# The first 70 microseconds of a streaming encoder step: conditions by 128-column blocks and another order of loads and engines

## The chip, the cores and the metric

The kernel runs on one core of a Trainium2 chip. A core has a matrix engine (TensorE, PE in the profile, with PEld for its weight loads), a vector engine (VectorE, DVE), an activation engine (ScalarE, ACT), GpSimd (POOL) and a sync engine (SyncE, SP). Each engine works through its own list of instructions in order, and the lists wait for one another by semaphores. DMA transfers are issued from the lists of SP, ACT or POOL and run on 16 shared DMA engines. The metric is the device time of one execution in microseconds; the kernel before takes 2170.99 us (median of 3 runs, 2169.61 to 2173.06).

## The reference

One step of a two-layer encoder in float32, for a prompt of 1024 frames and a sample of 32 frames that share the weights; the model width D is 1024.

```python
def rmsnorm(x, g):
    y = xf * lax.rsqrt(jnp.mean(xf * xf, axis=-1, keepdims=True) + EPS)
    return (y * g).astype(x.dtype)
...
for i in range(DEPTH):
    mod = jax.nn.silu(c) @ w_ada[i] + b_ada[i]
    sh1, sc1, gt1, sh2, sc2, gt2 = jnp.split(mod[:, None, :], N_MOD, axis=-1)
    h = rmsnorm(x, g_norm[i, 0]) * (1 + sc1) + sh1
    ...   # layer 0: z = gelu(h @ w_in), u and v are its halves, v is normalised and mixed over positions
    x = x + gt1 * rmsnorm(mix, g_norm[i, 1])
    h = rmsnorm(x, g_norm[i, 2]) * (1 + sc2) + sh2
    f = jnp.square(jax.nn.relu(h @ ffn_w_up[i])) @ ffn_w_down[i]
    x = x + gt2 * rmsnorm(f, g_norm[i, 3])
```

What matters here is the start of layer 0: the condition vector c (one for the prompt, one for the sample) gives a shift sh1 and a scale sc1 of 1024 entries each through a 1024 x 1024 block of w_ada; x is normalised, scaled and shifted to h; h is multiplied with w_in, whose second half gives v.

## The kernel before, in words

The 1056 rows are held transposed, features on the 128 partitions, in three tiles of 384, 384 and 288 columns (TILES). The 1024 features are eight blocks, written k = 0 to 7 here. Each float32 product of activations and weights is made of three products of split values: every weight tile is split into a high part (wh, by ScalarE, do_w, L422) and a low part (wl, by VectorE, L79 by the helper tt), the activations into hh and hl, and TensorE sums high-high, high-low and low-high.

All loads stand in one list, `stream`, and are issued by SP in that order as far as buffers are free (`issue`, L395 to L416). A weight item ("w") lands in one of three raw buffers; the x blocks ("x") and the first condition slices ("ada") have places of their own. `stream_to(kind, key)` works the list off up to an item: for a weight the split, for an x block the sum of squares on ScalarE (x_squares, L565) and eight 128 x 128 transposes on TensorE with copies out on VectorE or ScalarE (x_turn, L580 to L588), for a condition slice `do_ada_pe`. The list begins with x blocks 0 to 2, then four rounds q = 0 to 3, each with two half slices of the scale, two of the shift and one item of the weight for v, ("v", 0, q), which holds features 2q and 2q+1 for the first 512 columns of v. x blocks 3 to 5 follow the first round, 6 to 8 the last.

Conditions, in the prologue: a slice is 256 of the 6144 columns of w_ada, loaded in two halves of 512 KB (512 features by 256 columns). Slices 0 to 3 give the shift sh1, slices 4 to 7 the scale sc1. `do_ada_pe` (L472) multiplies them on TensorE with the Silu of c in four column groups of the array, and VectorE transposes the result in 32 x 32 blocks (L489, tile adas). A `fold`, called later, gathers it on TensorE with a small matrix (L459, tile adat) and lets VectorE add the bias and, for a scale, multiply with the gain (ada_finish, tiles shift and coef). TensorE, in order, stands at the gather until the transpose is done.

`first_norm` (L887) is a generator. Its first step makes the root of the mean square (spread, L715 to L727: a Sqrt by ScalarE, a reciprocal and a Newton step by VectorE), its second spreads it over the partitions with a diagonal (L730) and a matmul with ones (L732, tile pb_h) and copies it out (L893). Each further step (apply, L857) makes two blocks k of the modulated activations: mt (VectorE), hh (ScalarE, L875), hl (VectorE). Such a block needs scale and shift of its k.

The projection to v begins while all this runs: `early_mm` (L961, matmuls at L973) takes five blocks of 128 rows, three of the first tile (0, 1, 2) and two of the second (3, 4), and for each round q first the products with wh, then those with wl. The order of the whole prologue (from L991) is written out by hand in a `tc.manual_schedule()`. Its loop for q = 0 to 3: the next two k of tile 0, early_mm of blocks 0 to 2; in the first round x blocks 3 to 5 and the norm of tile 1; the next two k of tile 1; then `conditions(q + 1)` (both slices of the next round and the first fold), the next weight item, early_mm of block 3, the second fold, early_mm of block 4. After the loop come x blocks 6 to 8 (the third tile), its norm, and the sixth block; from there a planner orders the work.

The small vectors (gains, biases, c, pool scale, v's gain) are rows loaded by `load_vectors` on ScalarE's queue and turned by TensorE (turn_conditions for c, with Silu at L194; turn_vectors for the others, L206).

Later, v_rms makes the same kind of root for v's norm, once per tile, at L1067.

Of the kernel before, what the change touches and what calls it, by code (L numbers as in the profile page):

```python
# [15 lines left out]
P = 128  # L16
# [8 lines left out]
NV = 2  # L25
# [9 lines left out]
def tile_stream_encoder_step(  # L35
# [144 lines left out]
    def load_vectors(i, part):  # L180
        at = sum(k for _, k in rows[i][: part.start])
        for ap, k in rows[i][part]:
            nc.scalar.dma_start(vec_rows[i][at : at + k, :P], ap)
            at += k
# [6 lines left out]
    def turn_conditions():  # L191
# [4 lines left out]
        act(out=raw[0:16, 2 * P : 2 * P + 1], in_=epsT[0:16, :], func=AF.Sqrt)  # L196
# [50 lines left out]
    def add_wide(l, j):  # L247
# [10 lines left out]
                (2, 512),  # L258
            )
# [81 lines left out]
    for q in range(4):  # L341
# [3 lines left out]
        if q == 0:  # L345
            for b in range(3, 6):
                add_x(b)
# [33 lines left out]
    def in_raw(k):  # L381
        kind, key = stream[k][:2]
        return kind != "x" and not (kind == "ada" and k < first_ada)
# [11 lines left out]
    def issue():  # L395
        while state["issued"] < len(stream):
# [22 lines left out]
    def do_w(key, r):  # L419
# [4 lines left out]
        if key == ("v", 0, 0):  # L424
# [47 lines left out]
    def do_ada_pe(l, sl, q, r):  # L472
# [18 lines left out]
        def fold():  # L491
# [4 lines left out]
            )  # L496

# [111 lines left out]
    def stream_step():  # L609
# [6 lines left out]
        if kind == "w":  # L616
            do_w(key, r)
        elif kind == "wide":
# [96 lines left out]
    def spread(t, ss, tag, out, dg):  # L715
# [6 lines left out]
        act(out=r0[:, :nb], in_=ms[:, :nb], func=AF.Sqrt)  # L722
        nc.vector.reciprocal(out=r0[:, :nb], in_=r0[:, :nb])
# [129 lines left out]
    def apply(t, l, cf, sh, r, keep=False):  # L853
# [3 lines left out]
        if keep and len(segs[t]) == 1:  # L857
            parts = [parts[k] + parts[k + 1] for k in range(0, KB, 2)]
# [102 lines left out]
    def early_mm(bs, q):  # L961

        wh, wl = witem[("v", 0, q)]
        for second in (False, True):
            for b in bs:
                t, c0 = b // 3, b % 3 * P
                tick(0.46 if second else 0.92)
                for k in range(2):
                    kb = 2 * q + k
                    a_h, a_l = hh[t][:, kb, c0 : c0 + P], hl[t][:, kb, c0 : c0 + P]  # L970
                    w = slice(k * 512, k * 512 + 512)
                    for a in (a_h,) if second else (a_h, a_l):
                        mm(  # L973
                            early_ps[b],
                            a,
                            (wl if second else wh)[:, w],
                            start=kb == 0 and a is a_h and not second,
                            stop=kb == KB - 1 and second,
                        )
# [5 lines left out]
    def conditions(q):  # L985

        stream_to("ada", (0, 4 + q, 1))
        stream_to("ada", (0, q, 1))
        pe_folds.pop(0)()

    with tc.manual_schedule():  # L991
# [682 lines left out]
```

## Time and profile before

| | before |
|---|---|
| median of 3 runs | 2170.99 us (2169.61 to 2173.06) |
| profiled execution, whole time | 2173.74 us |
| its span, first to last instruction | 2171.7 us |
| granted TensorE clock, mean over the span | 0.996 |
| instructions | 33210 |
| HBM traffic over the span | 143 GB/s |

The profile is one execution. In lists of instructions a line reads: start, duration, engine, source line, operation, output<-inputs, form, count, and in brackets the idle time of the engine before it and what ended that. In the chain of waits a line is start, duration and what ran; "issue" is time in which nothing that the profile shows was waited for. In groups, the number after the bar is the busy time and the mean of one in ns, behind the second bar the idle time before them. In rows of stages the stretch is followed by its length, the busy time of PE, PEld, DVE, ACT and POOL with the number of instructions, the granted clock, the mean busy share of the DMA engines and GB/s. A row of waits is: engine and line, what it waited for, total us, times, longest. A row of DMA issues ends with KB of each and the median time to landing.

### The profile page before, as it was taken

Reading aid. Unit: us, or ns where it says so; the run is one execution under the profiler, and the core shown is the slowest. Engines: PE = TensorE matmul, PEld = TensorE weight load, DVE = VectorE, ACT = ScalarE, POOL = GpSimd, SP = SyncE. Lnnn points to the kernel's source line nnn. Section 1 sums busy time; section 2 is a strip of 40 time slices with the busy share of each in tenths; the row PEclk is TensorE's granted clock in tenths of the full one; section 3 lists DMA queues with packets and bytes.
Section 4 is the critical chain, followed back from the end, with each engine's and each line's share of the span. In section 5 each row is a group of like instructions: output and inputs, shape, how many; then the busy total and the mean of one; then the engine's idle time right before and its main releaser. Section 6 shows DMA issues by size and latency. Waiting matters only on the chain.

```text
span 2171.7 us, 33210 instructions
## 1 busy us (share of the span) xinstructions
PE 2145.5 (99%) x13214; PEld 2078.1 (96%) x13214; DVE 1431.8 (66%) x2499; ACT 971.3 (45%) x1643; POOL 13.3 (1%) x30
## 2 busy tenths in 40 slices
PE   7999999999999999999999999999999999999998
PEld 5778899999999999999999999999999999999997
DVE  5688647566879548496747879869675554523377
ACT  4633422234447552323445566666555542313354
POOL 0000000000000000000000000000000000000001
PEclk9999999999999999999999999999999999999999
DMA  8386534343437454243645466565455552302255
GB/s 300 119 269 193 173 93 139 90 148 109 147 96 233 132 155 143 87 140 110 196 129 161 141 189 182 171 191 158 141 161 158 157 155 68 98 20 78 69 139 125
DMA packets 383262, 312.95 MB, mean 144 GB/s; under 512 B 39458, under 2 KB 346346, under 8 KB 383108
## 3 DMA queue, kind: packets, MB, share of 16 engines
q1 hardware_dynamic: 380452, 308.64, 46.8%
q8 instruction: 103, 1.69, 0.3%
q10 hardware_dynamic: 2144, 1.41, 0.2%
q0 software_dynamic: 512, 0.79, 0.1%
q14 instruction: 51, 0.42, 0.1%
HBM read 278.95 MB, written 31.84 MB: 143 GB/s over the span
## 4 chain that ended last, share of the span: by engine, by line
PE 93%; DVE 3%; DMA 2%; ACT 1%; issue 1%; ACTq 0%; DVEq 0%; SPq 0%
PE pg L902 11%; PE pg L903 11%; PE pg L904 11%; PE pf L902 11%; PE pf L904 11%; PE pf L903 11%; PE po L902 3%; PE po L903 3%; PE po L904 3%; PE pu L902 3%; PE pu L904 3%; PE pu L903 3%; PE pv L929 2%; PE pv L930 2%; PE pv L931 2%; PE pp L1532 1%
## 5 line engine op out<-in xcount | busy, mean ns | idle before, releaser
L902 PE MATMUL pg<-fh,wh_dn 128*128 128x384 f32 (+1 forms) x1536 | 495.8, 323 | 0.0
L902 PE MATMUL pf<-hh,wh_up 128*128 128x384 f32 (+1 forms) x1536 | 494.4, 322 | 0.0
L903 PE MATMUL pf<-hl,wh_up 128*128 128x384 f32 (+1 forms) x1536 | 493.1, 321 | 0.0
L904 PE MATMUL pf<-hh,wl_up 128*128 128x384 f32 (+1 forms) x1536 | 492.9, 321 | 0.2 <-DVE wl_up L79 0.2
L903 PE MATMUL pg<-fl,wh_dn 128*128 128x384 f32 (+1 forms) x1536 | 492.6, 321 | 0.4 <-DVE fl L79 0.4
L904 PE MATMUL pg<-fh,wl_dn 128*128 128x384 f32 (+1 forms) x1536 | 492.5, 321 | 0.0
L79 DVE TENSOR_TENSOR wl_up<-raw,wh_up 128x1024 fp32r<-128x1024 f32 x152 | 185.9, 1224 | 165.4 <-ACT wh_up L422 165.4
L902 PEld LDWEIGHTS pg<-fh,wh_dn 128*128 128x128 f32 x1536 | 288.3, 188 | 1.5 <-ACT fh L1121 0.6
L903 PEld LDWEIGHTS pg<-fl,wh_dn 128*128 128x128 f32 x1536 | 288.3, 188 | 1.5 <-DVE fl L79 0.7
L904 PEld LDWEIGHTS pf<-hh,wl_up 128*128 128x128 f32 x1536 | 288.6, 188 | 0.5 <-DVE wl_up L79 0.5
L903 PEld LDWEIGHTS pf<-hl,wh_up 128*128 128x128 f32 x1536 | 288.3, 188 | 0.4
L902 PEld LDWEIGHTS pf<-hh,wh_up 128*128 128x128 f32 x1536 | 288.2, 188 | 0.4
L904 PEld LDWEIGHTS pg<-fh,wl_dn 128*128 128x128 f32 x1536 | 288.3, 188 | 0.0
L422 ACT ACTIVATE wh_up<-raw 128x1024 fp32r<-128x1024 f32 x152 | 161.2, 1060 | 279.9 <-PE pf L903 213.6
L79 DVE TENSOR_TENSOR acc<-acc,pg 128x384 f32<-128x384 f32 (+1 forms) x336 | 174.2, 519 | 146.3 <-PE pg L904 145.7
L422 ACT ACTIVATE wh_dn<-raw 128x1024 fp32r<-128x1024 f32 x152 | 160.8, 1059 | 202.9 <-PE pg L903 170.6
L79 DVE TENSOR_TENSOR wl_dn<-raw,wh_dn 128x1024 fp32r<-128x1024 f32 x152 | 186.0, 1224 | 82.4 <-ACT wh_dn L422 82.2
L79 DVE SCALAR_TENSOR_TENSOR aa<-raw,csil,aa 128x512 f32<-128x512 f32 (+1 forms) x364 | 203.5, 623 | 8.0 <-DMA raw<-in_w_ada_dram 7.9
L1295 ACT ACTIVATE r<-pf 128x384 f32<-128x384 f32 (+1 forms) x192 | 86.6, 451 | 201.9 <-PE pf L904 199.2
L79 DVE TENSOR_TENSOR fl<-r,fh 128x384 fp32r<-128x384 f32 (+1 forms) x192 | 100.3, 523 | 85.4 <-ACT fh L1121 84.3
L902 PE MATMUL pu<-hh,wh_u 128*128 128x384 f32 (+1 forms) x384 | 125.8, 328 | 0.0
L902 PE MATMUL po<-ush,wh_o 128*128 128x384 f32 (+1 forms) x384 | 123.5, 322 | 0.0
(263 smaller groups left out, 2927.2 us busy)
## 6 DMA issues: line engine op xcount, KB each, us to landing
raw<-in_ffn_w_up_dram SPq DMA_DIRECT2D x152, 512.0 KB, 3.9
raw<-in_ffn_w_down_dram SPq DMA_DIRECT2D x152, 512.0 KB, 3.5
raw<-in_w_ada_dram SPq DMA_DIRECT2D x96, 512.0 KB, 4.3
raw<-in_sgu_w_in_dram SPq DMA_DIRECT2D x40, 512.0 KB, 4.4
xd<-acc SPq DMA_DIRECT2D x8, 1536.0 KB, 7.8
raw<-in_sgu_w_out_dram SPq DMA_DIRECT2D x24, 512.0 KB, 4.0
xo_r<-xd SPq DMA_DIRECT2D x32, 384.0 KB, 3.4
vd<-vt SPq DMA_DIRECT2D x32, 256.0 KB, 4.5
```

The costliest lines, as they stand in the source:

```text
L79: return op(out, *args, **kw)
L422: act(out=wh, in_=r, func=AF.Copy)
L902: mm(ps[:, :n], wh, rh, start=i == 0, stop=False)
L903: mm(ps[:, :n], wh, rl, start=False, stop=False)
L904: mm(ps[:, :n], wl, rh, start=False, stop=i == last)
L929: mm(ps[:m, :], a_h, wh[:, o : o + 512], start=k == 0, stop=False)
L930: mm(ps[:m, :], a_h, wl[:, o : o + 512], start=False, stop=False)
L931: mm(ps[:m, :], a_l, wh[:, o : o + 512], start=False, stop=k == KB - 1)
L1295: act(out=r[:, :n], in_=ps[:, :n], func=AF.Relu)
L1532: mm(ps[:, :n], wg[:, k, e * P : (e + 1) * P], A(t, 2 * g + k), start=k == 0, stop=k == 1)
```

## The change

It touches the prologue up to the third tile's norm, and one line of v_rms.

- Shift and scale of k = 0 and k = 1 come from four blocks of 128 columns (columns 8, 0, 9, 1, each one load of 512 KB with all 1024 features), in place of slices 4 and 0. A new function, do_col, multiplies such a block.
- The order of loads: x 0 to 2; columns 8 and 0; ("v", 0, 0); columns 9 and 1; round 1; x 3 to 5; rounds 2 and 3; x 6 to 8. x block 2 is issued by SP instead of ScalarE's queue.
- g_norm, b_ada, pool_scale and sgu_g_v are issued by GpSimd's queue; c_prompt and c_sample stay on ScalarE's. A Silu of one column stands before the real one.
- Sqrt and reciprocal become Abs_reciprocal_sqrt, in spread and in v_rms.
- apply takes k = 0 and k = 1 one at a time. The low parts of all four items of v's first columns are made when the order calls for them (late_lo).
- The hand-written order is another one, and early_mm takes a list of k and either the products with wh or those with wl.

```diff
-    def load_vectors(i, part):
+    def load_vectors(queue, i, part):
...
-        act(out=raw[0:16, 2 * P : 2 * P + 1], in_=epsT[0:16, :], func=AF.Sqrt)
+        act(out=raw[0:16, 2 * P : 2 * P + 1], in_=epsT[0:16, :], func=AF.Abs_reciprocal_sqrt)
...
-    for q in range(4):
+    add_col(KB)
+    add_col(0)
+    add_w(*v_item(0, 0))
+    add_col(KB + 1)
+    add_col(1)
+    for q in range(1, 4):
         for j in (8 + 2 * q, 9 + 2 * q, 2 * q, 2 * q + 1):
             add_ada(0, j)
         add_w(*v_item(0, q))
-        if q == 0:
+        if q == 1:
             for b in range(3, 6):
                 add_x(b)
...
-                i = (nc.scalar if key == 2 else nc.sync).dma_start(
+                i = nc.sync.dma_start(
...
-        if key == ("v", 0, 0):
+        if key[:2] == ("v", 0):
...
+    def do_col(l, f, r):
+        pa = ps_ms(f"ada{l}_c{f}")
+        for k in range(KB):
+            c = k % 4
+            mm(
+                pa[32 * c : 32 * c + 32, :P],
+                csil32[:, k, :],
+                r[:, k * P : (k + 1) * P],
+                start=k < 4,
+                stop=k >= 4,
+                tile_position=(0, 32 * c),
+                skip_group_check=True,
+            )
+        s = t_m(f"adas{l}_c{f}")
+        nc.vector.transpose(out=s[:, :P], in_=pa[:, :P])
...
-        act(out=r0[:, :nb], in_=ms[:, :nb], func=AF.Sqrt)
-        nc.vector.reciprocal(out=r0[:, :nb], in_=r0[:, :nb])
+        act(out=r0[:, :nb], in_=ms[:, :nb], func=AF.Abs_reciprocal_sqrt)
...
-            parts = [parts[k] + parts[k + 1] for k in range(0, KB, 2)]
+            parts = parts[:2] + [parts[k] + parts[k + 1] for k in range(2, KB, 2)]
...
     with tc.manual_schedule():
-        load_vectors(2, slice(0, 2))
+        load_vectors(nc.scalar, 2, slice(0, 2))
         issue()
...
+        load_vectors(nc.gpsimd, 0, slice(0, 1))
+        load_vectors(nc.gpsimd, 1, slice(0, 1))
+        load_vectors(nc.gpsimd, 2, slice(2, 4))
+        act(out=vec_rows[2][64:80, P : P + 1], in_=epsT[64:80, :], func=AF.Silu)
         turn_conditions()
...
+        stream_to("x", 2)
         turn_vectors()
         next(h0)
+        column(KB)
+        fold()
+        column(0)
         statistics(h0)
+        fold()
         stream_to("w", ("v", 0, 0))
+        next(h0)
+        early_mm(front, (0,), False)
+        late_lo.pop()()
+        column(KB + 1)
+        early_mm(front, (0,), True)
+        fold()
+        column(1)
+        fold()
+        next(h0)
+        early_mm(front, (1,), False)
+        early_mm(front, (1,), True)
+        slice_(5)
+        fold()
+        slice_(1)
+        fold()
+        stream_to("w", ("v", 0, 1))
+        next(h0)
+        early_mm(front, (2, 3), False)
+        late_lo.pop()()
+        early_mm(front, (2, 3), True)
+        stream_to("x", 5)
+        turn_x()
+        next(h1)
+        slice_(6)
+        statistics(h1)
+        fold()
+        next(h1)
+        next(h1)
+        early_mm(rear, (0, 1), False)
+        early_mm(rear, (0, 1), True)
+        slice_(2)
+        fold()
+        stream_to("w", ("v", 0, 2))
+        next(h0)
+        next(h1)
+        early_mm(front, (4, 5), False)
+        late_lo.pop()()
+        early_mm(rear, (2, 3), False)
+        early_mm(rear, (2, 3), True)
+        early_mm(front, (4, 5), True)
+        next(h1)
+        slice_(7)
+        fold()
+        slice_(3)
+        fold()
+        early_mm(rear, (4, 5), False)
+        early_mm(rear, (4, 5), True)
+        stream_to("w", ("v", 0, 3))
+        next(h0)
+        next(h1)
+        early_mm(front, (6, 7), False)
+        late_lo.pop()()
+        early_mm(rear, (6, 7), False)
+        early_mm(front, (6, 7), True)
+        early_mm(rear, (6, 7), True)
         stream_to("x", 8)
...
-        act(out=x, in_=m, func=AF.Sqrt)
-        nc.vector.reciprocal(out=x, in_=x)
+        act(out=x, in_=m, func=AF.Abs_reciprocal_sqrt)
```

`column(f)` works the list off up to column f, `slice_(s)` up to the second half of slice s, `fold()` calls the oldest fold that is open, `turn_x()` turns the x blocks that are waiting; `front` is (0, 1, 2), `rear` is (3, 4).

More of the change, by code (lines that the diff above doesn't have):

```diff
@@ L258, in add_wide, with add_col @@
                 (2, 512),
+            )
+        )
+    def add_col(f):
+        stream.append(
+            (
+                "col",
+                (0, f),
+                w_ada[0][:, f * P : (f + 1) * P].rearrange("(k p) f -> p k f", p=P),
+                (8, P),
             )
@@ L382, in in_raw @@
         kind, key = stream[k][:2]
-        return kind != "x" and not (kind == "ada" and k < first_ada)
+        return kind not in ("x", "col") and not (kind == "ada" and k < first_ada)
     x_rows = [
@@ L617, in stream_step @@
             do_w(key, r)
+        elif kind == "col":
+            do_col(*key, r)
         elif kind == "wide":
```

85 lines of the change are left out of this document (32 added, 53 removed).

## The prediction

> **What bounds the kernel now.** I read the page first, then the busy time by stages, then the chain of waits and each engine's instructions in order for the first 90 us, because the diff touches nothing later except one root per tile.
>
> ```profile
> span 2171.7 us, 33210 instructions
> PE 2145.5 (99%) x13214; PEld 2078.1 (96%) x13214; DVE 1431.8 (66%) x2499; ACT 971.3 (45%) x1643; POOL 13.3 (1%) x30
> ...
> 0.00:19.77 19.77, 11.08 (x82) 7.84 (x82) 9.55 (x50) 9.59 (x18) 0.69 (x6) 0.99 0.87 306
> 19.77:68.20 48.43, 45.02 (x294) 32.03 (x295) 27.81 (x57) 21.12 (x38) 0.00 (x0) 0.90 0.64 222
> 68.20:87.00 18.80, 17.11 (x87) 13.61 (x86) 8.14 (x16) 13.96 (x28) 0.00 (x0) 1.00 0.41 135
> 87.00:125.00 38.00, 38.00 (x168) 30.84 (x167) 37.48 (x106) 16.82 (x44) 0.00 (x0) 1.00 0.57 175
> ```
>
> TensorE (PE) is busy for 99% of the span, and without a gap from 87 us on. So a microsecond by which the front of the kernel ends earlier or later goes straight to the end. The columns of the stage rows are the stretch, its length, the busy time of PE, PEld, DVE, ACT and POOL, the granted clock, the DMA share and GB/s. The change is worth what it does up to 68.20 us, where the transposes of the third x tile start in both kernels (the code behind that point is the same). Between the first projection matmul at 19.77 and that point TensorE idles only 48.43 - 45.02 = 3.4 us, but it does not run at full clock:
>
> ```profile
> 15.89:19.30 3.41, 1.93 (x34) 1.32 (x30) 1.82 (x6) 2.02 (x5) 0.00 (x0) 1.00 1.03 416
> 19.30:26.13 6.83, 6.36 (x14) 4.75 (x15) 3.27 (x9) 4.47 (x9) 0.00 (x0) 0.50 1.08 385
> 26.13:32.95 6.82, 5.50 (x47) 4.46 (x49) 2.08 (x3) 2.94 (x7) 0.00 (x0) 1.00 1.08 389
> 32.95:36.37 3.42, 1.70 (x37) 0.88 (x29) 3.01 (x7) 2.19 (x4) 0.00 (x0) 1.00 1.08 388
> 36.37:39.78 3.41, 3.41 (x16) 2.26 (x17) 1.93 (x5) 0.00 (x0) 0.00 (x0) 0.50 1.09 381
> 39.78:68.20 28.42, 28.06 (x192) 19.68 (x191) 17.69 (x36) 12.00 (x20) 0.00 (x0) 1.00 0.33 107
> ```
>
> A stretch of 3.41 us in which TensorE was busy 1.93 or 1.70 us is followed by half clock; 6.82 us with 5.50 busy is not. Half clock holds for 6.36 + 3.41 = 9.8 us of the stage and so costs about 4.9 us. DMA runs full (share over 1.0) until 39.78 and is light after that: the loads bound the start, TensorE and its waits bound the rest.
>
> **The start.** The first projection matmul waits for this chain: rows of c, Silu, x transposes, the norm's root, its broadcast, the split of the first weight, hh.
>
> ```profile
> 4.50 0.32 ACTq L183 DMA_DIRECT2D row<-in_b_ada_dram  x1
> 4.85 1.28 ACT L194 ACT_TABLE_LOAD   x1 [4.85 <-DMA x_rows<-in_x_prompt_dram]
> 6.15 0.31 ACT L194 ACTIVATE row<-row 16x128 f32<-16x128 f32 x1
> ...
> 6.79 3.68 PE L580 MATMUL xT<-ident,x_rows 128*128 128x128 f32 x16
> 10.39 1.18 PE L206 MATMUL rowT<-ident,row 64*128 64x64 f32 x3
> 11.50 1.97 PE L580 MATMUL xT<-ident,x_rows 128*128 128x128 f32 x8
> ...
> 19.77 0.79 PE L973 MATMUL pv<-wh_v,hh 128*128 128x512 f32 x1 [1.85 <-ACT hh L875]
> ...
> 30.09 1.07 PE L732 MATMUL pb_h<-r_h,ones 128*128 128x128 f32 x6 [0.98 <-ACT r_h L730]
> ...
> SPq L414 <- DMA row<-in_c_sample_dram: 2.7, 1, 2.7
> ...
> 14.12 0.16 DVE L79 TENSOR_SCALAR ms_h<-ssx 128x3 f32<-128x3 f32 x1
> 14.55 0.18 DVE L723 RECIPROCAL r_h<-r_h 128x3 f32<-128x3 f32 x1 [0.27 <-ACT r_h L722]
> ...
> 15.15 0.16 DVE L79 SCALAR_TENSOR_TENSOR r_h<-q_h,r_h 128x3 f32<-128x3 f32 x1
> ```
>
> Before, ScalarE (ACT) issues six small loads and one x block until 4.82, and only then loads the Silu table (1.28). After, it issues two, then touches Silu on spare data, so the table is there when c lands. SyncE (SP), which waits 2.7 us for c_sample (a load of another queue holds it up), has its next issue at 4.8, so I put c's landing there. Silu then starts at 4.8 instead of 6.15: 1.35 us. Three x blocks at 1.84 us each (3.68 for two) and the vectors (1.18) follow in one piece: 5.2 + 5.5 + 1.2 = 11.9, where x ended at 13.47 before (5.2 is Silu's 0.31 and 0.1 for the small transpose behind 4.8). The root took 14.12 to 15.31, 1.2; without the reciprocal (0.18) it takes 1.0 and ends at 12.9 instead of 15.31. From there to the first matmul I keep 19.77 - 15.31 = 4.46 us: broadcast, copy, split of v(0,0), hh. So the first matmul starts at 17.4: **-2.4 us**. The loads no longer decide it: 2.5 MB stand ahead of v(0,0)'s 0.5 MB instead of 3.5 MB. Bounds: -1.3 (only the table is gained) and -4.0 (the chain behind the root shortens too, since only one of eight blocks of hh is needed and the clock may rise earlier).
>
> **Work moved behind the start.** Columns 9 and 1 are now multiplied after the first matmul. A pair of 256-column slices takes 1.85 (row 45.60 below), a 128-column block a quarter of it: 2 x 0.46; two more gathers at 0.2 (0.24 and 0.26 in the same rows, overlapping what follows): **+1.3 us**. The other work is the same: 3 x 40 projection matmuls (one of three rows is shown), six slices, 24 transposes, one broadcast.
>
> ```profile
> L973 PE MATMUL pv<-wh_v,hh 128*128 128x512 f32 x40 | 18.8, 471 | 1.9 <-ACT hh L875 1.9
> ```
>
> **New waits of TensorE.** This is where the change costs. Before, a pair of slices is multiplied, the first gather follows (VectorE's transpose of the first slice ran under the second), then 6 matmuls of block 3, the second gather, 6 of block 4, and only then the front blocks that need the new shift. After, five gathers (slices 5, 1, 2, 7, 3) and column 1's stand directly behind their own matmuls, and for k = 1, 2-3 and 4-5 the front blocks follow with nothing in between. The chain of before shows what each piece lasts:
>
> ```profile
> 32.67 0.39 ACT r_h L893
> ...
> 35.45 0.45 DVE adas L489
> 35.90 0.14 issue
> 36.04 0.24 PE adat L459 x5
> ...
> 39.03 0.26 PE adat L459 x8
> ...
> 39.32 0.16 DVE shift L79
> 39.48 0.54 DVE mt L79
> ...
> 40.04 0.63 ACT hh L875
> ...
> 40.69 0.63 DVE hl L79
> ...
> 41.37 4.24 PE pv L973 x17
> 45.60 1.85 PE ada L477 x30
> ```
>
> (a) A gather behind its own slice: an estimated 0.2 for the last matmul to drain, 0.45, 0.14: 0.8 us, five times 4.0; column 1 with a transpose of half the width 0.65. Sum 4.7. (b) From a shift's gather to the first matmul, 39.29 to 40.69: 1.4, three times 4.2. For slices 7 and 3 the 12 matmuls of blocks 3 and 4 (12 x 0.23 = 2.8 by 4.24 for 17 with their waits) cover it; without that cover it would be 1.4 more. (c) hl 0.68 behind hh, of which 0.25 is covered by one matmul: 0.4 at six places, 2.6. (d) The second tile's norm has slice 6 alone beside it instead of the third x block's transposes: 1.0 for its diagonal (0.98 at 30.09), 1.7 from broadcast to hh (copy 0.39, mt 0.54, hh 0.63 and hand-overs), 0.9 for its second k (mt and hh again, less one matmul): 3.6. In all 15.1, in place of 3.4: **+11.7 us**. What queues behind each of these waits is the whole of TensorE's order; VectorE and ScalarE have 20 and 27 us to spare in the stage, so they do not become the bound. Bounds: 10 (half of the gathers find their transpose done) and 18 (every hl and x transpose waits as well).
>
> **Clock.** Four of these groups (k = 1, slices 5 and 1, the second norm, slice 2) leave 2.4 to 4.4 us idle within 5 to 7 us each, less busy than the two stretches that were followed by half clock. Four half-clock stretches would cost up to 6.8, none would save the 4.9 of before. I take the measured loss again: **0**, bounds -4.9 and +7.
> [...]
>
> **At nothing.** Small vectors by GpSimd: four issues from 1.3 us on at an estimated 0.6 each and a landing of 3.0, by the nearest row (late in the kernel, 48 KB each), end near 7 us; they are needed at 10.7 and hidden by the x transposes. If they land as late as w_ada in a full queue (8.0), they come at 11.8 and delay the start by 1.1; if not, nothing is gained. The four column loads have rows of 512 bytes in place of 1 KB; 4 MB stand up to column 1, which at the 306 GB/s of the first stage land by about 15 us, and TensorE reaches column 9 near 20 us, so they are covered; a third slower (the four of them 2 MB, some 7 us, then 9) would use half of the cover up. The roots of the v norm swap one table function for another: both need a table beside Gelu.
>
> ```profile
> raw<-in_w_ada_dram SPq DMA_DIRECT2D x20, 512.0 KB, 8.0
> ...
> out_dram<-turned POOLq DMA_DIRECT2D x16, 48.0 KB, 3.0
> ...
> L1067 ACT ACT_TABLE_LOAD x3 | 3.8, 1283 | 0.1
> L799 ACT ACT_TABLE_LOAD x3 | 3.8, 1283 | 0.1
> ```
>
> The first of the table rows is the old root's load, the second the new function's elsewhere in this kernel: three loads stay three (0, bounds -1 and +1 on ScalarE, off the path).
>
> **Sum.** -2.4 + 1.3 + 11.7 + 0 = +10.6 us. The profiled execution took 2173.74 (span 2171.7 and 2.0 around it) and would take 2184.3. It lies 2.75 above the median of the runs, 2170.99; against that median the forecast is **2181.6 us**. 0.2% (4.3 us) is about what a measurement of this kernel can tell from no change.
>
> **Rivals.**
> *The gathers are free (faster).* Place: TensorE between 17 and 60 us. If earlier loads let VectorE and ScalarE run ahead, so that (a) and (b), 8.9 us, are hidden, 6.2 remain, +2.8; and with so few holes the clock stays full, -4.9. With the early start of -4.0: -4.0 + 1.3 + 2.8 - 4.9 = -4.8, 2166.2. It decides once the stalls stay under about 6. For it: VectorE is idle 43% of the stage, and the DMA share of 1.08 up to 32.95 lets earlier loads matter. Against it: a gather needs its own slice's transpose, and a shift's chain can't start earlier. 0.14.
> *The stalls are there, the clock stays full.* 10.6 - 4.9 = +5.7, 2176.7. [...] Against it: the rows 15.89 and 32.95. 0.15.
> *GpSimd's loads are late.* +1.1 on top, 2182.7. Place: the transposes of the vectors in TensorE's queue ahead of column 8. Against it: 3.0 in the POOL row. 0.07.
> [...]
> *The stage's end absorbs it (no change).* 68.20 to 87.00 holds 1.7 us of idle TensorE, and VectorE is 37.48 of 38 us busy behind it: were VectorE the bound there, part of a delay would vanish, and with -4.0 at the start and 10 of stalls, -4.0 + 1.3 + 6.6 - 1.7 = +2.2, 2173.2. Against it: VectorE's work there hangs on loads that shift along. 0.09.
> *As forecast*, 0.55, by itself 2176 to 2190.
>
> **How the numbers follow.** Slower by over 0.2%: forecast 0.55, full clock 0.13 of its 0.15, GpSimd 0.07: 0.75. Within: 0.09 + 0.02 = 0.11. Faster: 0.14. The range 2168 to 2190 leaves out most of the faster case and the upper bounds of stalls and clock (+18 and +7), together under 0.2.
>
> **What would show it.** First projection matmul near 17.4 us; single idle pieces of 0.6 to 0.9 before gathers released by VectorE's adas, and of about 1.4 before matmuls released by hh; TensorE idle near 15 us up to the third tile's transposes, which start near 79 instead of 68.2; half clock in at least three stretches behind 20 us; the rest of the kernel unchanged. The forecast is wrong if these transposes start before 70 us, or if TensorE's idle time there is under 7 us.

## The result and the profile after

| | before | after |
|---|---|---|
| median, lowest to highest (4 runs each, same chip) | 2172.02 us, 2169.61 to 2174.28 | 2186.11 us, 2184.41 to 2189.55 |
| ratio after to before | | 1.0068, 95% interval 1.0055 to 1.0081 |
| profiled execution, whole time | 2173.74 us | 2184.41 us |
| first projection matmul | 19.77 us | 17.55 us |
| third tile's transposes begin | 68.20 us | 81.13 us |

The kernel became slower by 14.1 us (difference of the medians). The two profiled executions differ by only 10.7, because before's lies 1.7 above its median and after's 1.7 below. Page and stages of after:

```profile
span 2182.6 us, 33310 instructions
...
PE 2150.1 (99%) x13262; PEld 2081.4 (95%) x13262; DVE 1433.1 (66%) x2498; ACT 971.2 (44%) x1644; POOL 15.3 (1%) x34
```

```profile
0.00:17.55 17.55, 8.68 (x82) 7.33 (x82) 8.66 (x48) 9.74 (x18) 2.87 (x10) 1.00 0.89 290
17.55:81.13 63.58, 52.28 (x343) 35.71 (x344) 29.71 (x62) 21.61 (x38) 0.00 (x0) 0.84 0.52 184
81.13:99.93 18.80, 17.65 (x91) 14.23 (x90) 8.72 (x17) 14.60 (x29) 0.00 (x0) 1.00 0.43 139
99.93:137.93 38.00, 38.00 (x168) 30.72 (x167) 35.89 (x103) 16.95 (x43) 0.00 (x0) 1.00 0.57 170
```

The second row is where the time went. The stage from the first projection matmul to the third tile's transposes grew from 48.43 to 63.58 us. TensorE's idle time in it grew from 3.4 to 63.58 - 52.28 = 11.3 us, and its busy time grew too, from 45.02 to 52.28, at a lower granted clock (0.84, before 0.90). The work from 81.13 on is that of before from 68.20 on. TensorE's list shows most of the waits that make up the 11.3:

```profile
17.55 0.50 PE L1010 MATMUL pv<-wh_v,hh 128*128 128x512 f32 x1 [1.85 <-ACT hh L914]
...
23.68 0.24 PE L474 MATMUL adat_c<-adas_c,squares 128*32 128x2 f32 x8 [0.44 <-DVE adas_c L529]
25.38 0.79 PE L1010 MATMUL pv<-wh_v,hh 128*128 128x512 f32 x1 [1.46 <-ACT hh L914]
30.96 0.25 PE L474 MATMUL adat<-adas,squares 128*32 128x4 f32 x8 [0.57 <-DVE adas L504]
32.72 0.24 PE L474 MATMUL adat<-adas,squares 128*32 128x4 f32 x8 [0.56 <-DVE adas L504]
34.42 0.49 PE L1010 MATMUL pv<-wh_v,hh 128*128 128x512 f32 x1 [1.46 <-ACT hh L914]
35.08 0.50 PE L1010 MATMUL pv<-wh_v,hl 128*128 128x512 f32 x1 [0.16 <-DVE hl L79]
45.43 1.07 PE L771 MATMUL pb_h<-r_h,ones 128*128 128x128 f32 x6 [0.80 <-ACT r_h L769]
48.39 0.50 PE L1010 MATMUL pv<-wh_v,hh 128*128 128x512 f32 x1 [1.71 <-ACT hh L914]
50.22 0.79 PE L1010 MATMUL pv<-wh_v,hh 128*128 128x512 f32 x1 [0.53 <-ACT hh L914]
57.15 0.24 PE L474 MATMUL adat<-adas,squares 128*32 128x4 f32 x8 [0.58 <-DVE adas L504]
58.85 0.50 PE L1010 MATMUL pv<-wh_v,hh 128*128 128x512 f32 x1 [1.46 <-ACT hh L914]
69.52 0.24 PE L474 MATMUL adat<-adas,squares 128*32 128x4 f32 x8 [0.57 <-DVE adas L504]
71.27 0.24 PE L474 MATMUL adat<-adas,squares 128*32 128x4 f32 x8 [0.56 <-DVE adas L504]
...
98.84 0.50 PE L969 MATMUL pv<-wl_v,hh 128*128 128x512 f32 x1 [1.05 <-DVE wl_v L79]
```

A wait before adat is a gather behind its own slice (adat_c: its own column). A wait of 1.46 before an hh matmul is a chain from a fresh shift to the first matmul that uses it: shift 0.16, mt 0.54, hh 0.62 and hand-overs. Three more waits for hl of 0.15, at 18.21, 49.04 and 59.50, aren't shown; with them the waits of the stage sum to 11.3. The first wait, 1.85, lies before the stage and is as long as before. The last row lies behind the stage; its wait was 1.59 before.

Cut along the edges of the half-clock stretches, the stage shows the second loss:

```profile
11.68:15.10 3.42, 2.31 (x47) 1.60 (x47) 2.48 (x12) 1.19 (x4) 0.00 (x0) 1.00 1.11 365
15.10:18.51 3.41, 1.41 (x14) 0.88 (x14) 1.75 (x4) 1.94 (x3) 0.00 (x0) 1.00 1.10 378
...
18.51:21.93 3.42, 3.42 (x22) 2.08 (x21) 1.09 (x2) 0.00 (x0) 0.00 (x0) 0.50 1.09 392
21.93:25.34 3.41, 1.55 (x35) 0.78 (x33) 1.33 (x5) 0.63 (x2) 0.00 (x0) 1.00 1.05 413
25.34:28.75 3.41, 3.37 (x7) 2.44 (x8) 0.62 (x1) 0.93 (x1) 0.00 (x0) 0.50 1.05 389
...
32.17:35.58 3.41, 1.24 (x11) 0.64 (x11) 2.85 (x7) 1.83 (x3) 0.00 (x0) 1.00 1.07 390
...
35.58:38.99 3.41, 3.41 (x9) 2.71 (x9) 1.11 (x1) 2.66 (x6) 0.00 (x0) 0.50 1.10 383
...
42.41:45.82 3.41, 2.61 (x31) 1.78 (x29) 2.12 (x7) 2.13 (x6) 0.00 (x0) 1.00 0.75 237
45.82:49.23 3.41, 1.55 (x15) 1.02 (x14) 1.76 (x5) 1.25 (x3) 0.00 (x0) 1.00 0.01 2
49.23:52.65 3.42, 2.90 (x6) 1.77 (x6) 0.90 (x2) 1.56 (x2) 0.00 (x0) 0.50 0.00 0
52.65:56.06 3.41, 3.41 (x18) 1.92 (x20) 0.00 (x0) 0.00 (x0) 0.00 (x0) 0.50 0.00 0
...
56.06:59.47 3.41, 1.25 (x21) 0.34 (x9) 2.30 (x6) 1.15 (x2) 0.00 (x0) 1.00 0.00 0
59.47:62.89 3.42, 3.39 (x8) 2.71 (x9) 3.27 (x6) 1.15 (x2) 0.00 (x0) 0.50 0.00 0
```

In after's front each full-clock stretch of 3.41 us with 1.24 to 1.55 us of work is followed by half clock; those with 2.31 and 2.61 are not (other runs draw the line elsewhere, see the last section). A half-clock stretch with 2.90 us of work is followed by another, one with 3.37 or more by full clock. In all 19.9 us of work ran at half clock (3.42 + 3.37 + 3.41 + 6.31 + 3.39), which costs half of it, 9.9; before it was 9.8 of work, 4.9 lost. The difference is 5.0 us. That half clock costs half of the work is an estimate, from the granted clock of 0.50 in these rows. One pair of profiles shows the price: before and root_only (below) have the same order and nearly the same idle time, with 9.8 and 0 us at half clock, and 45.02 and 40.95 us of busy time. That is 4.1 us for 9.8, and at this rate the difference would be 4.2.

The clock is recorded only from 15.89 us in before and from 11.69 in after, and the 1.00 of a row ahead of that is no measurement. After's x transposes took 0.22 us each at 6.10 (5.38 for 24) and 0.13 each at 81.13 (2.04 for 16), so by these two figures I estimate that the first of them ran at half clock too.

**The account up to the transposes:** start 17.55 - 19.77 = -2.2; idle +7.9; clock +5.0; moved work +1.3 (the prediction's figure). Sum +12.0, measured 81.13 - 68.20 = +12.9. The 0.9 left over (1.7 with the smaller price of the clock) is in TensorE's busy time. The longer first matmul behind the new waits (0.50 or 0.79 beside a pace of 0.23 within a row of matmuls) is of that size, some 1.5 us by the working under (c) below, but no run isolates it.

**Behind it** the lag stays: 98.84 against 86.67 is +12.2 (the wait for wl_v has shrunk by 0.5), the last matmul 2172.28 against 2160.75 is +11.5, the span +10.9. Between these points the lag changes by less than 1 us each time.

### The profile page after: what moved, and what is told of

Same layout as the page of the kernel before. It is cut to its first block, busy times and chain, and to the rows that moved or that the text cites. A ratio compares the mean times of both kernels' runs of the same rounds, so it can differ in the third digit from the quotient of the medians.

```text
span 2182.6 us, 33310 instructions
## 1 busy us (share of the span) xinstructions
PE 2150.1 (99%) x13262; PEld 2081.4 (95%) x13262; DVE 1433.1 (66%) x2498; ACT 971.2 (44%) x1644; POOL 15.3 (1%) x34
## 4 chain that ended last, share of the span: by engine, by line
PE 95%; DVE 2%; DMA 2%; ACT 1%; issue 0%; DVEq 0%; ACTq 0%
PE pf L941 11%; PE pg L941 11%; PE pf L943 11%; PE pg L942 11%; PE pf L942 11%; PE pg L943 11%; PE po L941 3%; PE po L942 3%; PE po L943 3%; PE pu L941 3%; PE pu L943 3%; PE pu L942 3%; PE pv L969 2%; PE pv L968 2%; PE pv L970 2%; PE pv L1010 2%
```

## The experiments

All runs in one table. Times are in us. The idle time and the half clock are TensorE's between the first projection matmul and the third tile's transposes, in the profiled execution. The median stands beside that of the kernel before on the same chip; the ratio has its 95% interval.

| kernel | first matmul | transposes | idle | half clock | median / before | ratio |
|---|---|---|---|---|---|---|
| before | 19.77 | 68.20 | 3.4 | 9.8 | | |
| after | 17.55 | 81.13 | 11.3 | 20.5 | 2186.11 / 2172.02 | 1.0068 (1.0055 to 1.0081) |
| head_only | 18.46 | 64.47 | 3.7 | 3.4 | 2168.82 / 2172.43 | 0.998 (0.9971 to 0.9989) |
| head_again | 18.37 | 64.52 | 3.7 | 3.4 | 2167.84 / 2170.14 | 0.9992 (0.9983 to 1.0001) |
| root_only | 19.97 | 64.58 | 3.7 | 0 | 2170.66 / 2170.16 | 0.9996 (0.9988 to 1.0005) |
| head_act | 21.02 | 67.94 | 3.5 | 5.8 | 2171.46 / 2170.16 | 1.0004 (0.9995 to 1.0013) |
| head_warm | 18.88 | 63.15 | 3.5 | 0 | 2167.72 / 2170.16 | 0.999 (0.9981 to 0.9999) |
| folds_later | 17.14 | 76.23 | 8.6 | 17.1 | 2183.49 / 2172.43 | 1.0047 (1.0035 to 1.006) |
| warm | 16.81 | 76.02 | 1.0 | 3.4 | 2181.98 / 2172.43 | 1.0046 (1.0033 to 1.006) |
| covered | 17.36 | 66.70 | 4.3 | 6.8 | 2171.74 / 2172.43 | 0.9999 (0.999 to 1.0008) |
| covered2 | 17.78 | 61.30 | 1.5 | 0 | 2167.46 / 2170.16 | 0.9986 (0.9977 to 0.9995) |
| covered2_warm | 17.73 | 61.14 | 1.4 | 0 | 2164.57 / 2170.14 | 0.9973 (0.9963 to 0.9983) |

The theory tested first: the new head (queues, table, root, loads of c) is a gain of some 2 us, and the order behind it costs about 13, about 8 in waits and about 5 in clock. The rival: the head or the roots cost something too, or the columns and loads do, so that no order could win the time back.

### The head alone: head_only, head_again

The kernel before with the change's small loads, early Silu, x block 2 on SP and roots; the column loads and the order stay those of before.

```diff
-        load_vectors(2, slice(0, 2))
+        load_vectors(nc.scalar, 2, slice(0, 2))
         issue()
-        load_vectors(2, slice(2, 4))
-        load_vectors(0, slice(0, 1))
-        load_vectors(1, slice(0, 1))
+        load_vectors(nc.gpsimd, 0, slice(0, 1))
+        load_vectors(nc.gpsimd, 1, slice(0, 1))
+        load_vectors(nc.gpsimd, 2, slice(2, 4))
+        act(out=vec_rows[2][64:80, P : P + 1], in_=epsT[64:80, :], func=AF.Silu)
         turn_conditions()
-        stream_to("x", 1)
-        turn_vectors()
         stream_to("x", 2)
+        turn_vectors()
```

> The kernel before with the new head alone: the Silu table touched early, the four small vectors by GpSimd's queue, x block 2 by SP, one root function; slices, loads behind x and the order of all engines as before. Theory (the head is a gain, the order behind it is the loss): the first projection matmul comes 1 to 2.5 us earlier than 19.77 and the third tile's transposes by the same, so 1 to 3 us faster than before (2169 to 2171). Rival (GpSimd's queue or the root costs time): the first projection matmul not earlier than 19.8, and not faster than before.

> The new head on the order of before, unchanged from its first run, beside the run above on one chip. Theory (columns and loads are worth about nothing once the order covers them): ratio to before 0.997 to 0.999 again, 0 to 3 us above the run with spare matmuls. Rival (the third order is better by itself): more than 3 us above it.

TensorE's two waits for condition loads in head_only, then the stage:

```profile
13.60 0.64 PE L477 MATMUL ada<-raw,csil 128*32 128x256 f32 x8 [0.81 <-DMA raw<-in_w_ada_dram]
14.89 0.64 PE L477 MATMUL ada<-raw,csil 128*32 128x256 f32 x8 [0.66 <-DMA raw<-in_w_ada_dram]
```

```profile
18.46:64.47 46.01, 42.35 (x295) 30.16 (x296) 27.64 (x56) 21.13 (x38) 0.00 (x0) 0.96 0.68 240
```

The first matmul starts 1.3 us earlier than before, limited now by loads (0.81 and 0.66). The median is 3.6 us lower the first time and 2.3 the second; the two intervals overlap, and the second just reaches 1, so the head is worth some 2 to 4 us by the medians. The rival that the head costs something falls. head_again missed what was expected of it: its ratio is 0.9992, and it lies 3.3 us above covered2_warm (below) on one chip, where at most 3 was expected and more was to mean that the third order is better by itself. This doesn't settle it: covered2_warm also has spare matmuls, and head_again has none.

### Which part of the head: root_only, head_act

root_only is the kernel before with the new root in both places and nothing else. head_act is head_only with the four small vectors on ScalarE's queue, behind the early Silu, in place of GpSimd's.

```diff
 root_only, against before
-        act(out=r0[:, :nb], in_=ms[:, :nb], func=AF.Sqrt)
-        nc.vector.reciprocal(out=r0[:, :nb], in_=r0[:, :nb])
+        act(out=r0[:, :nb], in_=ms[:, :nb], func=AF.Abs_reciprocal_sqrt)
...
 head_act, against head_only
-        load_vectors(nc.gpsimd, 0, slice(0, 1))
-        load_vectors(nc.gpsimd, 1, slice(0, 1))
-        load_vectors(nc.gpsimd, 2, slice(2, 4))
         act(out=vec_rows[2][64:80, P : P + 1], in_=epsT[64:80, :], func=AF.Silu)
+        load_vectors(nc.scalar, 0, slice(0, 1))
+        load_vectors(nc.scalar, 1, slice(0, 1))
+        load_vectors(nc.scalar, 2, slice(2, 4))
```

> The kernel before with the one root function in place of square root and reciprocal, in spread and in the v norm. Theory: 0.2 us less on VectorE in the chain ahead of the first projection matmul, nothing else, three table loads at the v norm as before: 0 to 0.4 us faster, no difference to be measured. Rival (the other table brings more table loads, or fewer): over 2 us either way, with a changed number of table loads.

> The new head on the kernel before, but with the four small vectors on ScalarE's queue behind the Silu that is made early, and not on GpSimd's. Theory (what the head gains is the early table and SP's earlier loads; GpSimd's queue is worth little): first projection matmul within 0.5 us of the head with GpSimd's queue (18.46), the time within 1 us of its 2168.8. Rival (taking the vectors off the queue that shares its slots with SP's loads is the gain): first projection matmul near 19.5 and time near 2172.

The roots bring nothing: the first matmul of root_only starts at 19.97 (before 19.77), the interval holds 1. Its stage is nevertheless 3.8 us shorter than in before's profile, with nearly the same idle time (3.7 against 3.4) in the same order:

```profile
19.97:64.58 44.61, 40.95 (x294) 29.00 (x295) 27.64 (x56) 21.14 (x38) 0.00 (x0) 1.00 0.68 237
```

Its clock is 1.00 there and before's 0.90. The runs of before itself show the same without a change of code: of its 33 runs on this chip the 15 with a mean granted clock of 0.998 took 2169.2 us on average, the 8 with 0.996 took 2173.1. So one order draws more or less half clock in different executions, and 3 to 4 us between two profiles may be that alone. In the clock records of before and after every stretch that ends by 39.78 us (before) or 62.89 us (after) lasts 3.41, 6.83 or 10.24 us. I take the place of their edges against the work for the likely reason; it was not varied by itself.

head_act missed: the gain of the head is gone. Its waits on TensorE, and SP's waits up to 12 us (waited for, total, times, longest):

```profile
14.42 0.64 PE L477 MATMUL ada<-raw,csil 128*32 128x256 f32 x8 [1.91 <-DMA raw<-in_w_ada_dram]
...
16.39 0.97 PE L477 MATMUL ada<-raw,csil 128*32 128x256 f32 x8 [1.33 <-DMA raw<-in_w_ada_dram]
```

```profile
SPq L414 <- DMA row<-in_g_norm_dram: 2.6, 1, 2.6
SPq L414 <- DMA x_rows<-in_x_prompt_dram: 2.0, 1, 2.0
```

SP, about to issue a large load, stands 2.6 us for the landing of a small row that it has no use for, exactly as it stood 2.7 us for c_sample before. In head_only its longest wait there is 0.9. The traces of before and after show why: the loads that SP and ScalarE issue up to 14 us land on eight semaphores between them (100 and 102 to 108 in before; 100, 102, 111 and 113 to 117 in after), and from the ninth on each load waits for the semaphore of the load eight places ahead of it. So before's w_ada load at 4.82 us waits for 103, that of c_sample. After's four loads by GpSimd use 103 to 106. In these programs each small row on ScalarE's queue thus takes one of eight places from the large loads. GpSimd's queue is what makes the head's gain (2.6 us at the first matmul, 21.02 to 18.46). The early table alone brings none: the small transpose behind Silu starts 1.4 us earlier in head_act than in before (5.17 against 6.60), but then TensorE waits 1.91 and 1.33 for the slices.

### The clock: warm, head_warm

warm is after with spare matmuls ahead of the waits: 6 to 18 products of a constant tile, 128 columns each, in each hole. Nothing reads their result.

```diff
+    def warm(n):
+        pt = ps_ms("warm")
+        for _ in range(n):
+            mm(pt[:, :P], onesr, onesr, start=True, stop=True)
...
         next(h0)
+        warm(16)
         early_mm(front, (1,), False)
         early_mm(front, (1,), True)
         slice_(5)
+        warm(8)
         fold()
         slice_(1)
+        warm(8)
         fold()
+        warm(16)
...
 head_warm, against head_only
             if q == 0:
+                warm(20)
                 late_lo.pop()()
```

> The changed kernel with spare matmuls of 128 columns on a constant (6 to 18 at a place, results unused) in TensorE's holes: before the first projection matmul, before the gathers, and before the matmuls that wait for hh. They add work and take no wait away. Theory (half clock, 20.5 us of it in the stage against 9.8 before, is caused by these holes and costs some 5 us): at least half of the half-clock stretches go, the third tile's transposes come 3 to 8 us earlier than 81.13. Rival (the clock falls for another reason, or the holes alone make the loss): as many half-clock stretches, and the time the same or up to 4 us longer by the spare matmuls.

> The new head on the kernel before, with 20 spare 128-column matmuls in TensorE's 1.85 us hole ahead of the first projection matmul. Theory (that hole starts the half clock behind it): no half clock between the first projection matmul and the second tile's norm, 1 to 3 us faster than the new head alone (2168.8). Rival (the loads bind there, what the clock gives is lost in the next wait): the time within 0.7 us of 2168.8 and a longer wait before the gather near 33.5 us or the transposes of x block 3.

The first group of spare matmuls in warm (0.125 us each), and its stage up to the end of the half clock:

```profile
14.89 2.00 PE L1038 MATMUL warm<-ones 128*128 128x128 f32 x16
```

```profile
16.81:46.30 29.49, 28.67 (x272) 22.11 (x271) 13.80 (x33) 10.82 (x21) 0.00 (x0) 1.00 1.02 371
46.30:50.40 4.10, 3.95 (x9) 2.96 (x10) 0.60 (x1) 0.89 (x1) 0.00 (x0) 0.58 0.00 0
```

Half clock is left in one stretch in place of six, and the transposes start at 76.02 instead of 81.13, 5.1 us earlier, although the spare matmuls shorten no wait. Of this, 0.7 is the first matmul (16.81) and 4.4 the stage. Five stretches fewer are worth, by the same estimate of half of 3.41 us each, about 5 x 1.7 = 8.5 us; the 122 spare matmuls within the stage take about 122 x 0.125 = 15 us, where the holes that they fill held 11.3 - 1.0 = 10.3, so they give back some 5. The balance, 3.5, is near the 4.4 measured: the half clock is a real part of the loss and of about the size in the account, and this cure is itself dear. The median falls by 4.1 (2186.11 to 2181.98; the two intervals just overlap). In head_warm the transposes come 1.3 us earlier than in head_only and the half clock is gone, but by the ratios (0.999 against 0.998 and 0.9992) it is not better than head_only: there is too little half clock left to win back.

### The waits: folds_later

After, with other work put between a slice and its gather. The chains from shift to hh stay as they are in front of k = 1, k = 2-3 and k = 4-5.

```diff
         slice_(5)
-        fold()
         slice_(1)
         fold()
+        fold()
...
-        early_mm(rear, (0, 1), True)
         slice_(2)
+        early_mm(rear, (0, 1), True)
         fold()
...
         slice_(7)
-        fold()
         slice_(3)
         fold()
-        early_mm(rear, (4, 5), False)
+        early_mm((3,), (4, 5), False)
+        fold()
+        early_mm((4,), (4, 5), False)
```

(Column 1 likewise moves ahead of three matmuls and of column 9's gather.)

> The changed kernel with each gather moved behind other work (column 9's and 1's behind both columns and three projection matmuls, slice 5's behind slice 1's multiplication, slice 2's behind four projection matmuls, 7's and 3's behind 3's multiplication and block 3). Theory (the gathers' waits are part of the loss): of 3.3 us of idle time before gathers about 2.3 go, the third tile's transposes come 2 to 4 us earlier than 81.13, 2 to 4 us faster than the changed kernel. Rival (gathers only pass a wait on, the next matmul waits for hh anyway): the idle time before hh grows by as much and the time stays within 1 us.

The stage, and the one gather that still waits:

```profile
17.15:76.23 59.08, 50.44 (x343) 34.42 (x343) 29.43 (x62) 21.61 (x38) 0.00 (x0) 0.86 0.56 198
```

```profile
31.27 0.25 PE L474 MATMUL adat<-adas,squares 128*32 128x4 f32 x8 [0.53 <-DVE coef L79]
```

Idle time falls by 2.7 (11.3 to 8.6): the gathers, 3.3 us in after, are nearly covered. The waits for hh (1.46 to 1.72, four of them) stay, and so do five half-clock stretches of six: with the large holes left, most of the clock loss is left too. The transposes come 4.9 us earlier, more than the 2 to 4 expected: 0.4 by the first matmul, 2.7 by the idle time and some 1.7 by the one stretch less. The median falls by 2.6, the ratios' intervals overlap; the trace carries this verdict more than the time. The profiled execution was the slowest of the five, and lost 1.7 more at half clock around 271 us, which after's did not.

### Another order for the change's pieces: covered, covered2, covered2_warm

covered keeps the head, the column loads and the order of loads of after, and covers each gather and each chain with matmuls of blocks whose operands are ready; the first core of it:

```diff
+        column(KB + 1)
+        column(1)
         early_mm(front, (0,), False)
         late_lo.pop()()
-        column(KB + 1)
-        early_mm(front, (0,), True)
         fold()
-        column(1)
         fold()
         next(h0)
-        early_mm(front, (1,), False)
-        early_mm(front, (1,), True)
+        early_mm(front, (0,), True)
         slice_(5)
-        fold()
+        early_mm(front, (1,), False)
         slice_(1)
         fold()
+        early_mm(front, (1,), True)
+        fold()
         stream_to("w", ("v", 0, 1))
         next(h0)
+        stream_to("x", 3)
+        turn_x()
         early_mm(front, (2, 3), False)
```

> Head, columns and loads of the changed kernel, with a third order from the first projection matmul on: each fold and each shift-to-hh chain has projection matmuls, slices or x transposes of other blocks behind it in TensorE's queue. Theory (the loads and columns are no loss, the order's holes are): first projection matmul near 17.6 us, idle time of the stage under 5 us, third tile's transposes at 63 to 68 us, time 2167 to 2173, at least as fast as before. Rival (the columns' or the loads' cost keeps TensorE waiting): waits on loads show in the stage, and the time stays above 2178.

It gave a time equal to before's. One hole was left:

```profile
53.98 0.79 PE L1010 MATMUL pv<-wh_v,hh 128*128 128x512 f32 x1 [2.70 <-ACT hh L914]
```

The second tile's k = 4 and 5 were made behind slice 3's fold, so block 3's matmuls waited 2.70 for them, and half clock followed (53.46 to 60.29). covered2 makes them ahead of slice 3:

```diff
         slice_(7)
         early_mm(rear, (0, 1), True)
+        next(h1)
         slice_(3)
...
         early_mm(rear, (2, 3), True)
-        next(h1)
         early_mm(rear, (4, 5), False)
```

> The third order once more, with one step moved: VectorE and ScalarE make blocks k = 4 and 5 of tile 1 ahead of slice 3's fold and not behind k = 6 and 7 of tile 0. In the run before, TensorE stood 2.70 us for them at 53.98, and 6.8 us of half clock began at 53.46. Theory (holes cost themselves and then the clock): both go, third tile's transposes 4 to 6 us earlier than in that run, 2166 to 2169, faster than the kernel before and than the new head alone (2168.8). Rival (VectorE is the bound there): the idle time turns up before another hh, and the time stays at 2171 to 2173.

```profile
10.39:13.80 3.41, 2.23 (x47) 1.43 (x45) 2.65 (x11) 0.86 (x4) 0.00 (x0) 1.00 1.11 369
13.80:17.21 3.41, 3.41 (x54) 2.79 (x46) 1.28 (x5) 1.75 (x5) 0.00 (x0) 0.50 1.13 365
...
17.78:61.30 43.52, 42.00 (x311) 28.98 (x312) 28.82 (x62) 21.36 (x38) 0.00 (x0) 1.00 0.74 266
```

1.5 us of idle time in place of 11.3, no half clock from the first matmul to the transposes, 19.8 us earlier at the transposes than after, and 2.7 below before (2167.46 against 2170.16). So neither columns nor loads nor the head cost the 14 us; the hand-written order did, that of TensorE's list and of what VectorE and ScalarE prepare for it. What recorded half clock is left up to there lies ahead of the first matmul, behind a stretch with 2.23 us of work. covered2_warm fills that hole with spare matmuls, whose result nothing reads:

```diff
         column(KB)
+        warm(10)
         fold()
...
         column(KB + 1)
+        warm(8)
         column(1)
```

> The mended third order with 18 spare 128-column matmuls in the two holes ahead of the first projection matmul (10 before column 8's gather, 8 between columns 9 and 1). Theory (what spreads the runs of one kernel over 5 to 7 us is the place of the clock's stretches against the front's holes): no half clock from 12 us to the end of the front, the median 1 to 2 us below the mended order's ratio to before (0.9986), so 2164 to 2167, and a spread of its runs of at most 4 us. Rival (the spread comes from elsewhere): ratio 0.998 to 0.999 and a spread of 5 us or more.

2164.57 us, 5.6 below before and the best version. Its eight runs lie within 3.6 us (2163.74 to 2167.30), those of covered2 within 5.2. By the medians the eighteen spare matmuls are worth as much as the head; the two intervals (0.9977 to 0.9995 and 0.9963 to 0.9983) overlap a little, and in the two profiles the transposes start only 0.2 us apart (61.30 and 61.14), so the gain itself is not shown beyond doubt. Against head_warm, the old order with a full clock in the stage, covered2 is no faster (2167.46 and 2167.72 on one chip). Columns against slices by themselves, in one and the same order, weren't tried.

## Why the prediction was right, and which terms were mis-sized

The forecast was +10.6 (2181.6 us, slower); measured were +14.1 by the medians and +10.7 between the profiled executions. The mechanism was right: TensorE waits behind its own small results, and the early start doesn't make up for it. Two terms were wrong in opposite directions, the idle time by 3.8 too much and the clock by 5.0 too little, and that they offset each other is luck.

- **The start**, forecast -2.4 at 17.4 us: measured -2.2 at 17.55. The ground given for it held in part only. The path foretold for after is the measured one: the load of c_sample, Silu, the x transposes, the root (ended at 13.66, forecast 12.9), and nothing on it waits for w_ada. But before's start did not hang on the chain that the prediction names. Its chain of waits (first line) runs through a slice's load, up to 16.16 us; after's (second line) has only the small row:

```profile
7.66 8.50 DMA raw<-in_w_ada_dram
```

```profile
1.37 4.00 DMA row<-in_c_sample_dram
```

  This fits what the pieces of the other chain brought by themselves. The Silu table, to which 1.35 was put down, brings nothing when the small rows stay with ScalarE (head_act, first matmul 21.02), and the root's 0.2 is not to be seen (root_only). What gains is that loads come out of the way: GpSimd's queue, costed at nothing, does it in head_only; how much of after's gain is that queue's and how much the column loads' no run separates.
- **Gathers behind their slices (a)**, forecast 4.7: measured 0.57 + 0.56 + 0.58 + 0.57 + 0.56 + 0.44 = 3.3. No run shows the 0.2 put down for the last matmul to drain: in after's chain of waits 0.02 or 0.03 us lie between the end of a slice's multiplication and its transpose (30.43 to 30.46, 32.19 to 32.22, 56.63 to 56.65).
- **From shift to hh (b)**, forecast three times 1.4: three times 1.46, 4.4 in all. Behind slices 7 and 3 nothing waits, as forecast.
- **hl behind hh (c)**, forecast six times 0.4: four waits of 0.15 or 0.16, 0.6 in all. The loss is there all the same: from the first matmul's start to the second's it is 0.65 or 0.66 at all six places (35.08 - 34.42 = 0.66), against a pace of 0.23 at full clock, at four of them, and of 0.43 at half clock, at two. That makes 4 x 0.43 + 2 x 0.22 = 2.2, but the profile counts 0.50 us or more for the single matmul ahead, not the 0.25 that was assumed, and so some 1.5 of it as busy time.
- **The second norm (d)**, forecast 3.6 (1.0 + 1.7 + 0.9): 0.80 + 1.71 + 0.53 = 3.0.
- **Waits together**, forecast 15.1 in place of 3.4, inside bounds of 10 to 18: the waits above sum to 11.3 (3.3 + 4.4 + 0.6 + 3.0), as does the idle time, so +7.9 instead of +11.7. Of the 3.8 between them, 2.0 are (c), most of which is busy time, 1.4 are (a) and 0.6 are (d); (b) came out 0.2 dearer.
- **The clock** is the step that failed: "I take the measured loss again: 0", measured +5.0 (+4.2 by the price from before and root_only). The prediction counted four groups of holes less busy than the two stretches of before that were followed by half clock, priced them at up to 6.8, and then let that stand against 4.9 of before. Counted by stretches of 3.41 us, before has three half-clock stretches (one of them cut by the stage's start) and after six, at an estimated 1.7 us each. Without five of them warm's stage is 4.4 us shorter, though its spare matmuls take some 5 us themselves.
- **The full-clock rival** (+5.7) falls with those rows: none of the full-clock stretches ahead of half clock was idle. They held 1.24 to 1.55 us of work in 3.41 in after, 1.70 and 1.93 in before.
- **Gathers free**: falls; a gather waited 0.56 in each place where nothing stood between, and idle stayed over 11 us.
- **GpSimd's loads late**: falls. No transpose of a row waited for them in after; only covered shows such a wait, 0.22. In the list of loads up to 17.55 us (KB, median us from issue to landing):

```profile
row<-in_b_ada_dram POOLq DMA_DIRECT2D x1, 48.0 KB, 6.6
row<-in_g_norm_dram POOLq DMA_DIRECT2D x1, 32.0 KB, 5.0
```

  The four took 5.0 to 6.8, not the 3.0 of the nearest row of before, and were hidden all the same.
- **The end absorbs it**: at the place named the lag shrank by 0.8 (81.13 - 68.20 = 12.93 to 98.84 - 86.67 = 12.17), not by 1.7, and the start and the stalls that it also assumed came out dearer. TensorE is busy for all 38.00 us behind it while VectorE has fallen to 35.89, so VectorE is no bound there.
- **Table loads** at the v norm stay three, and the rest of the kernel changes little, as forecast (the lag falls from 12.9 to 10.9 over it).

The 14.1 of the medians is 3.4 more than the 10.7 on which the sum was made. The chance of clock edges is the likely cause: the four runs of after have mean granted clocks of 0.994, 0.992, 0.993 and 0.992 in the order 2184.41, 2189.55, 2185.11, 2187.12 us, the profiled one being the first. The 33 runs of before above show the same relation, 3.9 us between a clock of 0.998 and one of 0.996; that it explains these 3.4 was not tested by itself.

## What to carry to other kernels

On an engine that sets the end, the order of its list is worth more than earlier data: never put the consumer of a small result directly behind its producer, but work that is already ready between them (here 17 us lie between two orders of the same work, +14.1 and -2.7). Cost a hole twice, once as idle time and once as the half clock that may follow, counted in stretches of 3.41 us (an estimated 1.7 us each here), and give spare matmuls to a hole that can't be covered (here 2.9 us of median between covered2 and covered2_warm, each against before, not shown beyond doubt). Keep small loads off a queue that shares places with large ones (here SP stood 2.6 and 2.7 us for such rows), and compare orders by several runs, since the runs of before with a mean clock of 0.998 and of 0.996 lay 3.9 us apart.

## What the runs showed of the hardware that was not expected

- Half clock came without an idle stretch ahead of it, and busy time alone did not set its edge. Stretches of 3.41 us at full clock with as little as 0.81 us of work (head_act, from 13.14) and as much as 2.59 (warm, from 43.57) were followed by half clock; others with 1.69 (head_act, from 33.62) and 1.82 (before, from 84.15) were not. What sets it the runs leave open. The rows of before and of warm:

```profile
84.15:87.56 3.41, 1.82 (x9) 1.19 (x8) 2.70 (x6) 2.02 (x5) 0.00 (x0) 1.00 0.72 244
```

```profile
43.57:46.99 3.42, 2.59 (x17) 1.73 (x15) 1.96 (x4) 1.98 (x3) 0.00 (x0) 1.00 0.39 123
```

- What ended half clock is sharper: up to the last ten microseconds of each profile, a half-clock stretch with up to 3.04 us of work (folds_later) was followed by another one, one with 3.26 (head_only) or more by full clock.
- Spare matmuls may win more than they cost: 18 of them went with a median 5.6 us below before in place of 2.7, and a spread of 3.6 us in place of 5.2; the intervals of the two versions overlap a little.
- A small load held up large ones by its place alone: SP stood 2.6 us (head_act) and 2.7 us (before) for rows of 32 KB and 4 KB of another queue, and with the four small vectors on GpSimd's queue (head_only) it stood at most 0.9.
